# A hybrid decoder layer on one core: rows of x scaled before their transposes, dummy products ahead of the first unit, and two memory attention units moved between the heads of the differential attention

## The chip, the core and the metric

The kernel runs on one core of a Trainium2 chip. The core has a matrix engine (TensorE, PE in the profile, with its weight loads as PEld), a vector engine (DVE), a scalar engine (ACT), a general engine (POOL), and DMA queues issued mainly by SP. Each engine works through its own queue in order and waits on semaphores for the others. The metric is the device time of one launch in microseconds.

## The reference

One layer for 512 rows (tokens) of width 1024, in fp32. What the change touches is the beginning (the first norm and projection) and the two attention groups:

```python
h = rms_norm(x, attn_norm[l])
proj = h @ w_in[l]
q_da, k_da, v_da, rw_cols, q_mem = jnp.split(proj, [c1, c2, c3, c4], axis=-1)
...
o_da = diff_attention(q_da, k_da, v_da, positions, ...)     # 4 heads, 2 softmax maps each, causal
o_rw = rwkv7_time_mix(rw_cols, ...)                         # 4 heads, recurrent state
o_mem = memory_attention(q_mem, mem_n, w_mem_kv[l], ...)    # 4 heads on 256 memory rows
mixed = jnp.concatenate([o_da, o_rw.astype(o_da.dtype), o_mem], axis=-1)
x = x + mixed @ w_out[l]
xn = rms_norm(x, ffn_norm[l])
x = x + hierarchical_moe(xn, ...)                           # 16 experts of width 512
```

The norm is `x * rsqrt(mean(x*x) + eps) * gain`, by row.

## The kernel before

**Weights.** A stream (`WeightStream`) loads blocks of 512 KB into raw tiles; ACT rounds each to a high part (L96) and DVE subtracts it for a low part (L97). A product in fp32 accuracy is then three products of such parts (`mm3`, L243 to L245; in the first unit L341 to L343; in the output projection L1063 to L1065).

**The front.** x lies in four tiles `xt[0]` to `xt[3]` of 128 rows by 1024 (in the profile `f`). `row_root` gives 1/rms of each row: the sum of squares by DVE (L279) for tiles 0 and 2 and by ACT (L281) for tiles 1 and 3, then two POOL operations (L282, L283). DVE (tiles 0, 1, L348) and ACT (tiles 2, 3, L364) multiply the identity by the root, which gives a diagonal (in the profile `qmT`). `half_turn(n)` is two products of a 128x128 block of x with a diagonal (L328), which transpose and scale at once; n counts 16 half-blocks, the first 8 for tiles 0 and 1. They go to six PSUM banks, two half-blocks to a bank. `half_split(n)` reads a half-block into a high part (L291, ACT) and a low one (L292, DVE) with the norm's gain. `half_products` multiplies them with the first two weight blocks: 24 products of 128x256 for each group of four half-blocks. In this part the order on ACT, DVE and PE is the order in which it is written (`manual_schedule`); elsewhere a scheduler orders each engine's queue.

**The middle.** A weaver (`Weave`) interleaves generators by the costs that they yield: projections, the recurrence of RWKV (with a solve on DVE, L743 and L744, whose result goes through DRAM to the products L772), and attention.

**Attention.** `attention` runs through 20 units. A unit "d" is a block of 128 query rows of one head of the differential attention, in four sizes; a unit "m" is half the rows of a pair of memory heads, and a to d are the four of them. In step i the scores of unit i are issued, then the values of unit i−3, then the transposes of unit i−2. Scores of a memory unit are eight products (L949) into two PSUM banks `pp`, two reductions for the maxima (L952, DVE), four exponentials that read the banks (L956, ACT) and a scaling by POOL (L959). Its turn is eight transposes (L976) in two groups with a copy by ACT after each (L977), its values are four products (L1010). When a head is complete, its rows are normalized, transposed (L1003) and split (L291, L292). Then `out_first` begins the output projection (L1063 to L1065) in four `pp` banks; `give` hands two tiles of attention to the weight stream as further raw tiles. The 16 experts follow from about 340 us on.

Of the kernel before, what the change touches and what calls it, by code (L numbers as in the profile page):

```python
# [150 lines left out]
def hybrid_layer_kernel(ctx, tc, x, mem, positions, cols, w_in, w_kv, w_out, wa2, g2, ffn, wr, br,  # L151
# [22 lines left out]
    def pc():  # L174
        return pools["ps"].tile([P, 512], F32, name="pc", bufs=2)
# [18 lines left out]
    def b4(name, shape, dtype=F32):  # L194
        return biga.tile(shape, dtype, name=name)
# [79 lines left out]
    def row_root(src, vec=True):  # L275
        ss = wk.tile([P, 1], F32, name="ssx", bufs=4)
        r = wk.tile([P, 1], F32, name="rsx", bufs=4)
        if vec:
            V.tensor_tensor_reduce(b4("aw0", [P, D]), src, src, 1.0, 0.0, op0=ALU.mult, op1=ALU.add, accum_out=ss)  # L279
        else:  # L280
            A.activation(b4("aw1", [P, D]), src, AF.Square, accum_out=ss)  # L281
        G.tensor_scalar(r, ss, 1.0 / D, RMS_EPS, op0=ALU.mult, op1=ALU.add)  # L282
        return r, G.tensor_tensor(r, r, mhalf, op=ALU.pow)  # L283
# [9 lines left out]


    held = [ws.pair.pop() for _ in range(4)]
    ws.pump()
    for t in (2, 3):
        nc.sync.dma_start(xt[t], x[t * P:(t + 1) * P, :])
# [5 lines left out]
    dint = post_[:, S:2 * S]  # L304
    nc.sync.dma_start(posr, bass.AP(tensor=positions.tensor, offset=positions.offset, ap=[[0, P], [1, S]]))
    nc.sync.dma_start(posc, positions.rearrange("o (t p) -> p (o t)", p=P))
    diags = [b4(f"qmT{t}", [P, 2, P]) for t in range(2)]
    diag = [diags[t // 2][:, t % 2, :] for t in range(NT)]
    first_ps = [pp() for _ in range(2)]
    first_w = []  # L310

# [12 lines left out]
    def half_turn(n):  # L324
        hf, k = divmod(n, KC)
        o = half_bank(n)
        for t in range(2):
            T.matmul(o[:, t * P:(t + 1) * P], xt[2 * hf + t][:, k * P:(k + 1) * P], diag[2 * hf + t], start=True, stop=True)  # L328

    def half_split(n):  # L330
        hf, k = divmod(n, KC)
        tk = slice(hf * 256, hf * 256 + 256)
        return split_cols(half_bank(n), col[:, C_AN + k:C_AN + k + 1], h_hi[:, k, tk], h_lo[:, k, tk])
# [9 lines left out]
                T.matmul(o, wl, h_hi[:, k, tk], start=False, stop=k == KC - 1, skip_group_check=True)  # L343

    with tc.manual_schedule(engines={mybir.EngineType.Activation, mybir.EngineType.DVE, mybir.EngineType.PE}):
        roots = [row_root(xt[0]), row_root(xt[1], False)]
        for t in range(2):
            V.tensor_scalar(diag[t], ident, roots[t][0], None, op0=ALU.mult)  # L348
        for n in range(6):
            half_turn(n)  # L350
        weights()
        half_split(0)
        half_split(1)
        for n in (6, 7):
            half_turn(n)
        half_split(2)
        half_split(3)
        weights()
        roots += [row_root(xt[2]), row_root(xt[3], False)]
        half_products(0, range(4))  # L360
        for n in range(4, KC):
            half_split(n)
        for t in (2, 3):
            A.activation(diag[t], ident, AF.Copy, scale=roots[t][0])  # L364
        for n in range(KC, KC + 4):
            half_turn(n)
        half_products(0, range(4, KC))
        half_split(KC)
        half_split(KC + 1)
        for n in range(KC + 4, 2 * KC):  # L370
            half_turn(n)
        for n in range(KC + 2, 2 * KC):
            got_h = half_split(n)
        half_products(1, range(KC))
# [524 lines left out]
    def attention():  # L899
# [9 lines left out]
        aws = [b4("aw0", [P, 1024]), b4("aw1", [P, 1024])]  # L909
        obs = [b4("ob1", [P, S]), None]  # L910
        yield lambda: done[0] == 6
        units = [z for c in "0123abcd" for z in ([("d", int(c), qb) for qb in range(NT)] if c in "0123" else [("m", "abcd".index(c), 0)])]
        st = {}

        def scores(i):
# [102 lines left out]
            return None  # L1018

        n = len(units)  # L1020
        closes = {}
        for i in range(n + 3):
            if i == 1:
                yield has("bk_done")
                pr2 = b4("f0", [P, 2, 1024])
                prs[1:] = [pr2[:, k, :] for k in range(2)]
            elif i == 7:
                yield has("merged")
                obs[1] = b4("prod", [P, S])
            if i < n:  # L1030
                scores(i)
            if i == 15:
                with tc.high_priority(offset=GP):
                    ws.depth = 2 * DEPTH
                    give(("kT", 2), ("qT", 2))
                    ws.depth = DEPTH
            if i == n - 1:
                wv.spawn(out_first(), OUT_PRI)
            if i == 3:
                yield has("v0")  # L1040
            if i == 8:
                yield has("proj")
            if 0 <= i - 3 < n:
                cl = values(i - 3)
                if cl:
                    closes[i + 2] = cl
            if 0 <= i - 2 < n:
                turn(i - 2)
            if i in closes:
                closes.pop(i)()  # L1050
            yield (2.5 if i < 16 else 4.5)
        for k in sorted(closes):
            closes[k]()
        flags.add("att")
# [48 lines left out]
    with tc.issue_after(anchor[0].ins):  # L1103
# [4 lines left out]
        dum = rc.tile([P, 1], F32, name="dum")  # L1108
        G.iota(dum, pattern=[[0, 1]], base=S, channel_multiplier=1, allow_small_or_imprecise_dtypes=True)
        tri = rc.tile([P, P], BF, name="tri")  # L1110
        onb = rc.tile([P, P], BF, name="onb")
        G.memset(onb, 1.0)
        G.affine_select(tri, onb, pattern=[[1, P]], compare_op=ALU.is_gt, fill=0.0, base=0, channel_multiplier=-1)
        member = rc.tile([P, NT, NE], BF, name="member")
        rankm = rc.tile([P, NT, NE], F32, name="rankm")
# [387 lines left out]
```

## Time and profile before

| | us |
|---|---|
| median of 3 runs | 627.85 |
| lowest and highest | 626.47, 631.8 |
| the profiled execution | 631.21 |
| its span, first to last instruction | 629.5 |
| PE busy in it | 603.6 |
| DVE busy in it | 496.4 |
| ACT busy in it | 413.9 |

The rows of the trace come from one profiled execution. In a timeline row, the first number is the start and the second the duration in us, then engine, line, operation, output and inputs; x8 is a group of eight. In square brackets stands how long the engine was idle before it, and what ended that. PE's records overlap, so that a group's time divided by its count is a little more than the distance from one record to the next.

### The profile page before, as it was taken

The numbers are of one execution on the slowest core, as the hardware profiler recorded it, in microseconds if no ns is written. First come the engines' busy times: TensorE is split into PE (matmuls) and PEld (weight loads), VectorE is DVE, ScalarE is ACT, GpSimd is POOL, SyncE is SP. The second block draws the span as 40 slices with busy tenths as digits, with TensorE's granted clock in tenths as the row PEclk, the third lists the DMA queues.
The fourth block names the chain that finished last, engine by engine and source line by source line (L and its number), as shares of the span: only waits on it lengthen the run. The fifth ranks groups of instructions, "written<-read, shape, count | busy, mean of one in ns | idle before, by whom it ended". The sixth has DMA issues, their size and how long they took to land.

```text
span 629.5 us, 11197 instructions
## 1 busy us (share of the span) xinstructions
PE 603.6 (96%) x4130; PEld 486.6 (77%) x4130; DVE 496.4 (79%) x897; ACT 413.9 (66%) x633; POOL 124.0 (20%) x129
## 2 busy tenths in 40 slices
PE   4999999999999999999998999999999999999992
PEld 4968899999988877889996777777777777777771
DVE  5655795699966687555468999999999999988991
ACT  5478433453449675655247788888889888888881
POOL 2710211244400114304002011111011111320001
PEclk9999999999999997999999999999999999999997
DMA  9442333323252030879798999999999999799913
GB/s 303 137 137 67 101 101 98 87 70 99 68 118 69 2 135 1 298 272 348 278 336 278 364 345 371 372 373 355 364 356 361 363 364 373 232 373 375 337 26 54
DMA packets 77502, 144.19 MB, mean 229 GB/s; under 512 B 12832, under 2 KB 30496, under 8 KB 77440
## 3 DMA queue, kind: packets, MB, share of 16 engines
q1 hardware_dynamic: 69344, 126.59, 57.1%
q0 software_dynamic: 3760, 13.24, 8.9%
q10 hardware_dynamic: 4336, 3.57, 1.8%
q8 instruction: 34, 0.56, 0.4%
q14 instruction: 28, 0.23, 0.1%
HBM read 131.72 MB, written 11.67 MB: 228 GB/s over the span
## 4 chain that ended last, share of the span: by engine, by line
PE 82%; DVE 9%; DMA 3%; ACT 2%; issue 2%; POOL 1%; ACTq 0%; POOLq 0%; SPq 0%; DVEq 0%
PE pp L243 14%; PE pp L245 13%; PE pp L244 13%; PE py L244 5%; PE py L245 4%; PE py L243 4%; DVE prod L743 3%; DVE wlo L97 3%; PE pp L1063 3%; PE pp L1064 2%; PE pp L1065 2%; PE pt L986 2%; DVE lor L744 2%; PE pp L1345 1%; PE py L1201 1%
## 5 line engine op out<-in xcount | busy, mean ns | idle before, releaser
L245 PE MATMUL pp<-whi,xl 128*96 128x512 f32 x264 | 104.0, 395 | 0.0
L244 PE MATMUL pp<-wlo,xh 128*96 128x512 f32 x264 | 103.8, 394 | 0.0
L243 PE MATMUL pp<-whi,xh 128*96 128x512 f32 x264 | 101.2, 394 | 0.8 <-ACT xh L1332 0.8
L1393 POOL DMA_INDIRECT out<-ye,sidx x16 | 23.2, 1452 | 226.3 <-DVE gidx L1295 118.7
L96 ACT ACTIVATE whi<-raw 128x1024 fp32r<-128x1024 f32 x42 | 44.1, 1058 | 32.9 <-PE pp L245 24.7
L245 PE MATMUL pp<-whi,hm_l 128*128 128x256 f32 x224 | 63.8, 285 | 0.0
L243 PE MATMUL pp<-whi,hm_h 128*128 128x256 f32 x224 | 63.1, 282 | 0.0
L244 PE MATMUL pp<-wlo,hm_h 128*128 128x256 f32 x224 | 63.1, 282 | 0.0
L97 DVE TENSOR_TENSOR wlo<-raw,whi 128x1024 fp32r<-128x1024 f32 x42 | 53.7, 1284 | 11.2 <-ACT whi L96 10.8
L243 PEld LDWEIGHTS pp<-whi,xh 128*96 128x96 f32 x264 | 42.5, 161 | 19.6 <-ACT xh L1332 1.3
L245 PEld LDWEIGHTS pp<-whi,xl 128*96 128x96 f32 x264 | 42.6, 161 | 18.4
L244 PEld LDWEIGHTS pp<-wlo,xh 128*96 128x96 f32 x264 | 42.5, 161 | 18.2
L244 PE MATMUL py<-wlo,hh 128*96 128x512 f32 x120 | 47.9, 399 | 0.0
L245 PE MATMUL py<-whi,hl 128*96 128x512 f32 x120 | 47.0, 392 | 0.0
L243 PE MATMUL py<-whi,hh 128*96 128x512 f32 x120 | 47.0, 392 | 0.0
L97 DVE TENSOR_TENSOR wlo<-u,whi 128x1024 fp32r<-128x1024 f32 x34 | 40.8, 1224 | 6.2 <-ACT whi L96 6.1
L97 DVE TENSOR_TENSOR wlo<-lraw,whi 128x1024 fp32r<-128x1024 f32 x36 | 42.6, 1219 | 2.7 <-ACT whi L96 2.5
L245 PEld LDWEIGHTS pp<-whi,hm_l 128*128 128x128 f32 x224 | 42.1, 188 | 1.2 <-issue 0.5
L243 PEld LDWEIGHTS pp<-whi,hm_h 128*128 128x128 f32 x224 | 42.0, 188 | 1.0 <-DVE sm L936 0.4
L244 PEld LDWEIGHTS pp<-wlo,hm_h 128*128 128x128 f32 x224 | 42.3, 189 | 0.6 <-issue 0.2
L96 ACT ACTIVATE whi<-lraw 128x1024 fp32r<-128x1024 f32 x36 | 37.1, 1058 | 5.1 <-PE pp L245 3.6
L96 ACT ACTIVATE whi<-u 128x1024 fp32r<-128x1024 f32 x34 | 35.2, 1057 | 6.7 <-PE pp L1065 3.7
(405 smaller groups left out, 1568.5 us busy)
## 6 DMA issues: line engine op xcount, KB each, us to landing
raw<-in_w_in SPq DMA_DIRECT2D x22, 512.0 KB, 3.7
u<-in_wd SPq DMA_DIRECT2D x12, 512.0 KB, 9.4
lraw<-in_wg SPq DMA_DIRECT2D x12, 512.0 KB, 11.2
lraw<-in_wu SPq DMA_DIRECT2D x12, 512.0 KB, 7.5
lraw<-in_wd SPq DMA_DIRECT2D x12, 512.0 KB, 12.4
f<-in_wg SPq DMA_DIRECT2D x11, 512.0 KB, 10.0
u<-in_wu SPq DMA_DIRECT2D x11, 512.0 KB, 12.5
eraw<-in_wd SPq DMA_DIRECT2D x10, 512.0 KB, 13.5
```

Of the source, the lines that this page charges most:

```text
L96: nc.scalar.activation(hi, slot, AF.Copy)
L97: nc.vector.tensor_sub(lo, slot, hi.bitcast(F32))
L243: T.matmul(ps, ah, bh, start=first, stop=False)
L244: T.matmul(ps, ah, bl, start=False, stop=False)
L245: T.matmul(ps, al, bh, start=False, stop=last)
L743: V.tensor_mul(prod[:, :, 0:n], ud[:, s:s + 1, s:32].to_broadcast([P, 16, n]), zs[:, :, s:32])
L744: V.tensor_reduce(zs[:, :, s], prod[:, :, 0:n], axis=AX.X, op=ALU.add)
L986: T.matmul(po[:, 0:P], aws[i % 2][:, kb * P:(kb + 1) * P], qk["v"][:, kb, h * P:(h + 1) * P], start=kb == 0, stop=kb == qb)
L1063: T.matmul(o, ah, hi[:, k % 4, :], start=k == k0 and i == lead, stop=False, skip_group_check=True)
L1064: T.matmul(o, ah, lo[:, k % 4, :], start=False, stop=False, skip_group_check=True)
L1065: T.matmul(o, al, hi[:, k % 4, :], start=False, stop=k == k1, skip_group_check=True)
L1393: G.indirect_dma_start(out, bass.IndirectOffsetOnAxis(ap=si, axis=0), ye, None, compute_op=ALU.add)
```

## The change

Four things are changed. First, the two halves of each row of x are multiplied by the root in place (L354 by ACT for tiles 0 and 2, L355 by DVE for tiles 1 and 3), and `half_turn` is a transpose with the identity; the diagonals are gone. Second, 80 products of a 128x128 tile of ones in bf16 with itself (L348) stand at the head of PE's queue; nothing reads their result. The tile `onb` is set earlier on POOL for that. Third, the front's order: the roots of tiles 2 and 3 are written ahead of the second weight block's split, and the second half of the first half's products (`half_products(0, 4..7)`) ahead of the transposes 8 to 11. Fourth, the attention units go in the order 0, 1, a, 2, b, 3, c, d instead of 0, 1, 2, 3, a, b, c, d; the gift of `kT` and `qT` comes at the last unit "d" (step 17 instead of 15), and a step yields 2.5 for a unit "d" and 4.5 else. Lines behind the front are 7 to 9 higher after the change: L949 is L957, L976 is L984, L1010 is L1018, L1003 is L1011, L772 is L780, and L1063 to L1065 are L1072 to L1074.

```diff
--- before.py
+++ after.py
@@ -293,6 +293,8 @@
 
 
     held = [ws.pair.pop() for _ in range(4)]
+    onb = rc.tile([P, P], BF, name="onb")
+    G.memset(onb, 1.0)
     ws.pump()
     for t in (2, 3):
         nc.sync.dma_start(xt[t], x[t * P:(t + 1) * P, :])
@@ -304,8 +306,6 @@
     dint = post_[:, S:2 * S]
     nc.sync.dma_start(posr, bass.AP(tensor=positions.tensor, offset=positions.offset, ap=[[0, P], [1, S]]))
     nc.sync.dma_start(posc, positions.rearrange("o (t p) -> p (o t)", p=P))
-    diags = [b4(f"qmT{t}", [P, 2, P]) for t in range(2)]
-    diag = [diags[t // 2][:, t % 2, :] for t in range(NT)]
     first_ps = [pp() for _ in range(2)]
     first_w = []
 
@@ -325,7 +325,7 @@
         hf, k = divmod(n, KC)
         o = half_bank(n)
         for t in range(2):
-            T.matmul(o[:, t * P:(t + 1) * P], xt[2 * hf + t][:, k * P:(k + 1) * P], diag[2 * hf + t], start=True, stop=True)
+            T.transpose(o[:, t * P:(t + 1) * P], xt[2 * hf + t][:, k * P:(k + 1) * P], ident)
 
     def half_split(n):
         hf, k = divmod(n, KC)
@@ -343,28 +343,36 @@
                 T.matmul(o, wl, h_hi[:, k, tk], start=False, stop=k == KC - 1, skip_group_check=True)
 
     with tc.manual_schedule(engines={mybir.EngineType.Activation, mybir.EngineType.DVE, mybir.EngineType.PE}):
+        early = pc()
+        for _ in range(80):
+            T.matmul(early[:, 0:P], onb, onb, start=True, stop=True)
         roots = [row_root(xt[0]), row_root(xt[1], False)]
-        for t in range(2):
-            V.tensor_scalar(diag[t], ident, roots[t][0], None, op0=ALU.mult)
+
+        def half_scale(hf):
+            for i in range(2):
+                cs = slice(i * 512, i * 512 + 512)
+                A.activation(xt[2 * hf][:, cs], xt[2 * hf][:, cs], AF.Copy, scale=roots[2 * hf][0])
+                V.tensor_scalar(xt[2 * hf + 1][:, cs], xt[2 * hf + 1][:, cs], roots[2 * hf + 1][0], None, op0=ALU.mult)
+
+        half_scale(0)
         for n in range(6):
             half_turn(n)
         weights()
-        half_split(0)
-        half_split(1)
+        for n in range(2):
+            half_split(n)
         for n in (6, 7):
             half_turn(n)
-        half_split(2)
-        half_split(3)
+        for n in range(2, 4):
+            half_split(n)
+        roots += [row_root(xt[2]), row_root(xt[3], False)]
         weights()
-        roots += [row_root(xt[2]), row_root(xt[3], False)]
         half_products(0, range(4))
         for n in range(4, KC):
             half_split(n)
-        for t in (2, 3):
-            A.activation(diag[t], ident, AF.Copy, scale=roots[t][0])
+        half_scale(1)
+        half_products(0, range(4, KC))
         for n in range(KC, KC + 4):
             half_turn(n)
-        half_products(0, range(4, KC))
         half_split(KC)
         half_split(KC + 1)
         for n in range(KC + 4, 2 * KC):
@@ -909,7 +917,7 @@
         aws = [b4("aw0", [P, 1024]), b4("aw1", [P, 1024])]
         obs = [b4("ob1", [P, S]), None]
         yield lambda: done[0] == 6
-        units = [z for c in "0123abcd" for z in ([("d", int(c), qb) for qb in range(NT)] if c in "0123" else [("m", "abcd".index(c), 0)])]
+        units = [z for c in "01a2b3cd" for z in ([("d", int(c), qb) for qb in range(NT)] if c in "0123" else [("m", "abcd".index(c), 0)])]
         st = {}
 
         def scores(i):
@@ -1018,6 +1026,7 @@
             return None
 
         n = len(units)
+        last_d = max(i for i in range(n) if units[i][0] == "d")
         closes = {}
         for i in range(n + 3):
             if i == 1:
@@ -1029,7 +1038,7 @@
                 obs[1] = b4("prod", [P, S])
             if i < n:
                 scores(i)
-            if i == 15:
+            if i == last_d:
                 with tc.high_priority(offset=GP):
                     ws.depth = 2 * DEPTH
                     give(("kT", 2), ("qT", 2))
@@ -1048,7 +1057,7 @@
                 turn(i - 2)
             if i in closes:
                 closes.pop(i)()
-            yield (2.5 if i < 16 else 4.5)
+            yield 2.5 if i < n and units[i][0] == "d" else 4.5
         for k in sorted(closes):
             closes[k]()
         flags.add("att")
@@ -1108,8 +1117,6 @@
         dum = rc.tile([P, 1], F32, name="dum")
         G.iota(dum, pattern=[[0, 1]], base=S, channel_multiplier=1, allow_small_or_imprecise_dtypes=True)
         tri = rc.tile([P, P], BF, name="tri")
-        onb = rc.tile([P, P], BF, name="onb")
-        G.memset(onb, 1.0)
         G.affine_select(tri, onb, pattern=[[1, P]], compare_op=ALU.is_gt, fill=0.0, base=0, channel_multiplier=-1)
         member = rc.tile([P, NT, NE], BF, name="member")
         rankm = rc.tile([P, NT, NE], F32, name="rankm")
```

On PE, at the start of the program, there stood (`f` is x, `qmT` a diagonal, `pt`, `pc`, `pp` are PSUM banks, `whi` and `wlo` weights):

```order
L328 MATMUL pt<-qmT_132,f_96 128x128 x4
L328 MATMUL pc<-qmT_132,f_96 128x128 x4
L328 MATMUL pp<-qmT_132,f_96 128x128 x4
L328 MATMUL pt<-qmT_132,f_96 128x128 x4
L341 MATMUL pp<-hm_h,whi_80 128x256
L342 MATMUL pp<-hm_l,whi_80 128x256
```

and now stands, behind 78 more such products:

```order
L348 LDWEIGHTS onb
L348 MATMUL pc<-onb 128x128
L348 LDWEIGHTS onb
L348 MATMUL pc<-onb 128x128
L328 MATMUL pt<-ident,f_96 128x128 x4
L328 MATMUL pc<-ident,f_96 128x128 x4
L328 MATMUL pp<-ident,f_96 128x128 x4
L328 MATMUL pt<-ident,f_96 128x128 x4
L341 MATMUL pp<-hm_h,whi_80 128x256
L342 MATMUL pp<-hm_l,whi_80 128x256
```

The dummies are ahead of the transposes, which take the identity where the diagonal was.

On PE, around the scores of unit d (`mkT`, `qmT` are the memory's keys and queries), there stood:

```order
L949 MATMUL pp<-mkT_379,qmT_377 128x256 x3
L859 MATMUL pc<-f_990,u_648 64x64 x4
L845 MATMUL pc<-f_990,u_647 64x64 x8
L949 MATMUL pp<-mkT_379,qmT_377 128x256 x4
L854 MATMUL pc<-f_990,f_991 64x64 x4
L1003 MATMUL pt<-ident,ob_2004 128x128 x4
L986 MATMUL pt<-v_da,aw_2002 128x128 x3
L1063 MATMUL pp<-whi_85,hm_h 128x256
L1064 MATMUL pp<-wlo_86,hm_h 128x256
L1065 MATMUL pp<-whi_85,hm_l 128x256
L1063 MATMUL pp<-whi_80,hm_h 128x256
```

and now stands:

```order
L1018 MATMUL pt<-aw_2087,mv 64x256 x2
L1018 MATMUL pt<-aw_2088,mv 64x256 x2
L977 MATMUL pt<-ident,f_2251 128x128
L957 MATMUL pp<-mkT_464,qmT_462 128x256 x4
L862 MATMUL pc<-f_1075,f_1076 64x64 x4
L957 MATMUL pp<-mkT_464,qmT_462 128x256 x3
L994 MATMUL pt<-v_da,aw_2087 128x128
L977 MATMUL pt<-ident,pown 128x128 x2
L867 MATMUL pc<-f_1075,u_733 64x64 x4
L853 MATMUL pc<-f_1075,u_732 64x64 x8
L1072 MATMUL pp<-whi_85,hm_h 128x256
L1073 MATMUL pp<-wlo_86,hm_h 128x256
```

Of unit d's eight score products the last three now stand five rows ahead of the first output product (L1072), with small products of the recurrence and transposes of the last head (L977) in between; before, a head's transpose (L1003) and values (L986) stood there.

On PE, where units c and d are turned (`aw` is their transposed attention, `mv` the memory's values, L822 and L830 a transpose of the recurrence, `prod` a head's rows), there stood:

```order
L976 MATMUL pt<-ident,f_2166 128x128 x4
L1010 MATMUL pt<-aw_2002,mv 64x256 x2
L1010 MATMUL pt<-aw_2003,mv 64x256 x2
L976 MATMUL pt<-ident,pown 128x128 x4
L822 MATMUL pc<-ident,r_t 128x128 x4
L976 MATMUL pt<-ident,pown 128x128 x4
L1003 MATMUL pt<-ident,prod 128x128 x4
L1010 MATMUL pt<-aw_2002,mv 64x256 x2
L1010 MATMUL pt<-aw_2003,mv 64x256 x2
L1063 MATMUL pp<-whi_85,hm_h 128x256 x3
L1064 MATMUL pp<-wlo_86,hm_h 128x256 x3
```

and now stands:

```order
L830 MATMUL pc<-ident,r_t 128x128 x4
L994 MATMUL pt<-v_da,aw_2088 128x128 x4
L984 MATMUL pt<-ident,pown 128x128 x8
L1018 MATMUL pt<-aw_2087,mv 64x256 x2
L1018 MATMUL pt<-aw_2088,mv 64x256 x2
L984 MATMUL pt<-ident,f_2251 128x128 x8
L1018 MATMUL pt<-aw_2087,mv 64x256 x2
L1018 MATMUL pt<-aw_2088,mv 64x256 x2
L1011 MATMUL pt<-ident,prod 128x128 x4
L1072 MATMUL pp<-whi_85,hm_h 128x256 x4
L1073 MATMUL pp<-wlo_86,hm_h 128x256 x4
```

The turns and values of c and d and the closing transpose of the last head (L1011) are in one row, with output products only ahead of it and behind it.

## Rows read from the trace of the kernel before

**Rows 1.** The page: span, busy shares, TensorE clock by fortieths, last chain by engine

```profile
span 629.5 us, 11197 instructions
...
PE 603.6 (96%) x4130; PEld 486.6 (77%) x4130; DVE 496.4 (79%) x897; ACT 413.9 (66%) x633; POOL 124.0 (20%) x129
...
PEclk9999999999999997999999999999999999999997
...
PE 82%; DVE 9%; DMA 3%; ACT 2%; issue 2%; POOL 1%; ACTq 0%; POOLq 0%; SPq 0%; DVEq 0%
```

**Rows 2.** Waits of PE, 0 to 340 us: total, times, longest

```profile
PE pt L328 <- DVE qmT L348: 8.4, 2, 8.2
...
PE pc L772 <- DMA lor<-zs_d: 0.8, 1, 0.8
```

**Rows 3.** Timeline, 7 to 31 us: start, duration, engine, line

```profile
8.90 0.28 DVE L348 TENSOR_SCALAR qmT<-ident,rsx 128x128 f32<-128x128 f32 x1 [0.40 <-POOL rsx L283]
...
9.24 1.65 PE L328 MATMUL pt<-qmT,f 128*128 128x128 f32 x6 [0.21 <-DVE qmT L348]
...
9.57 1.23 DVE L97 TENSOR_TENSOR wlo<-raw,whi 128x1024 fp32r<-128x1024 f32 x1
10.07 0.47 ACT L291 ACTIVATE hm_h<-pt,col 128x256 fp32r<-128x256 f32 x1 [1.35 <-PE pt L328]
...
10.71 0.48 DVE L292 SCALAR_TENSOR_TENSOR hm_l<-pt,col,hm_h 128x256 fp32r<-128x256 f32 x1
...
13.74 1.06 PE L328 MATMUL pt<-qmT,f 128*128 128x128 f32 x8
...
14.56 0.36 PE L341 MATMUL pp<-hm_h,whi 128*128 128x256 f32 x1
...
23.14 1.05 PE L328 MATMUL pt<-qmT,f 128*128 128x128 f32 x8
...
30.46 0.28 PE L343 MATMUL pp<-hm_h,wlo 128*128 128x256 f32 x1
```

**Rows 4.** Two stretches of PE's timeline: a transpose group, and 128-column bf16 products

```profile
271.90 0.60 PE L976 MATMUL pt<-ident,f 128*128 128x128 f32 x4
...
321.83 0.66 PE L1269 MATMUL pp<-onb 128*128 128x128 bf16 x9
```

**Rows 5.** Groups by line and form, 186 to 290 us: count, busy us, mean ns

```profile
L977 ACT ACTIVATE aw<-pt 128x512 f32<-128x512 f32 x8 | 4.8, 595 | 1.5 <-PE pt L976 1.5
...
L1142 DVE TENSOR_TENSOR u<-pp,u 128x512 f32<-128x512 f32 x4 | 2.6, 684 | 3.2 <-PE pp L1065 3.2
```

**Rows 6.** Windows: PE, PEld, DVE, ACT, POOL busy (count), PEclk, DMA, GB/s

```profile
180.00:190.00 10.00, 9.21 (x101) 8.23 (x99) 4.88 (x18) 4.41 (x15) 1.04 (x2) 1.00 0.49 99
190.00:240.00 50.00, 50.00 (x611) 40.22 (x608) 38.00 (x123) 39.77 (x109) 6.83 (x9) 1.00 0.20 65
240.00:242.00 2.00, 0.89 (x10) 0.35 (x6) 1.97 (x5) 1.93 (x8) 1.58 (x1) 1.00 0.00 0
242.00:250.00 8.00, 8.00 (x44) 6.91 (x44) 4.80 (x15) 2.28 (x8) 2.86 (x2) 0.57 0.01 2
...
266.00:270.00 4.00, 3.34 (x26) 2.06 (x24) 3.01 (x7) 3.69 (x8) 0.00 (x0) 1.00 1.03 373
```

**Rows 7.** Timeline, 239 to 244 us, all engines

```profile
239.49 0.69 PE L845 MATMUL pc<-f,u 128*64 128x64 f32 x16
...
239.61 1.29 DVE L952 TENSOR_REDUCE mxm<-pp 128x2 f32<-128x512 f32 x2
...
239.99 0.47 ACT L956 ACTIVATE f<-pp,mxm 128x256 f32<-128x256 f32 x1
...
241.36 0.48 ACT L956 ACTIVATE f<-pp,mxm 128x256 f32<-128x256 f32 x1
...
243.94 0.93 PEld L854 LDWEIGHTS pc<-f,f 128*64 128x64 f32 x8 [0.65 <-DVE mxm L952]
```

**Rows 8.** Source view of L1063: count, duration min/median/max, first and last start

```profile
L1063 PE MATMUL pp<-xhi,hm_h x32: 276/276/364, 287.1 to 307.8; 128*128 128x256 f32 x32
```

## The prediction

> **What bounds the kernel now.** Read the page first [rows 1]: PE is busy 603.6 of 629.5 us, and 82% of the chain that ended last is PE. Then PE's waits [rows 2]: before 340 us the only long one is at the start, 8.2 us until the first diagonal L348; the next, 0.8 us, is at L772, for a DMA. So from about 14.5 us on the program is one long PE queue, and an edit is worth what it takes from that queue, from its few holes, or from stretches in which it runs at half pace. The rest is found in three places.
>
> The start [rows 3]: PE waits until the roots are known, then turns the first half of x by products with diagonals. [...] The first projection products run from 14.5 to 30.46 + 0.28 us. The end of attention [rows 6]: in 240–242 PE is busy 0.89 of 2 us; in 242–250 the granted clock is 0.57, so 0.43 × 8 = 3.4 us are lost; in 266–270 0.66 us are idle. And L772 [rows 6]: 180–190 has 0.79 us idle.
>
> **The change, part by part.** *Transposes for diagonal products.* A diagonal product of 128 columns leaves two records, a transpose one: 64 records become 32. Eight records of L328 take 1.05 us warm [rows 3]; four transposes of the same width take 0.60 [rows 4], and with the 0.27 us that the last one drains, that is 0.11 apart. Warm, 32 × 0.11 = 3.5 us leave PE's queue. At half pace, as the first 24 records ran, it is up to twice as much for those.
>
> *Scaling in place* takes the place of four 128-column diagonals. ACT: two halves of 512 columns at 0.60 (L977) [rows 5]. DVE: two at 0.69, from L1142, which reads two inputs of that size [rows 5]; four L348s of 0.28 [rows 3] would bound it above at 1.12 each, and below one diagonal itself, 0.28. I take 0.69, the nearest shape. The roots come as before, the second at 8.90, so the first transposes start at 8.90 + 0.69 = 9.6 instead of 8.2 and 9.24, and L97, which stood at 9.57, starts at 10.3 + and ends at 11.6.
>
> *The order of the front, by hand from these durations.* Transposes 0–5: 9.6 to about 11.1. Splits L291/L292 at 0.47 and 0.48 [rows 3] are now the limit: the first L292 follows L97 at 11.6, so the bank for transposes 6 and 7 is free at 12.6, and products 0–3 start at about 12.9, where before it was 14.5. They take 24 × 0.117 = 2.8 us, to 15.7. The square sum of x's third tile (taken as 1.23, L97's price for as many columns) and the second L97 stand on DVE ahead of splits 4–7, so products 4–7 wait until about 16.5 (0.8 us of new PE wait) and run to 19.3. DVE's second scaling ends there too; being ahead of transposes 8–11 on DVE but behind products 4–7 on PE, it is covered. Without that cover its 1.4 us would show. Sixteen transposes to 21.4, 48 products of 0.117 to about 27.1 + 0.5. Before, the last started at 30.46. The front gains **3.1 us**; 0.9 if the products run at half pace for a while (first rival), 3.7 if the transposes start at 9.2.
>
> *Eighty dummy products* of onb stand ahead of all this on PE. Warm, such products come (0.66 − 0.22)/8 = 0.055 apart [rows 4]; at half pace 0.11. PE begins near 1.5 us, as soon as POOL has made onb. All at full pace they take 4.4 us, half of them at each pace 40 × 0.11 + 40 × 0.055 = 6.6, to about 8.1, ahead of the first transpose at 9.6. All at half pace: 8.8 us, to 10.3, which delays the transposes by 0.7, of which the wait for L97 hides most. So they cost 0 to 0.5, taken as 0; what they give (full pace for transposes and products) is in the 3.1. The memset of onb was already there, and is moved on POOL ahead of nothing that waits.
>
> *The middle.* It is carried along by PE's queue. L772's wait for the solve's DMA may go or grow. In the new order L772 stands earlier by some 50 matmuls, but DVE has less to do during the solve (two weight splits and attention's first reductions come after it). I take the wait as gone: **−0.8**; bounds −0.8 and +3.1 (the front's whole gain waits there).
>
> *Memory units a and b among the heads, c and d at the end.* A unit's chain is two reductions (L952, 1.29 us for both) and four exponentials 0.47 apart (239.99 to 241.36 and 0.5 more) [rows 7], about 3.4 us before its two banks are free again. Before, four chains follow one another with little PE work between them, and this made the holes at 240–250. What may go: 1.1 (240–242), 0.65 (L854, waiting for L952 [rows 7]), 3.4 (half clock), 0.66 (266–270): **−5.8**. What comes: units a and b, each among score products of a head and the recurrence's small matmuls, which cover the chain wholly (0) or not at all (3.4); I take 0.7 each, near the low end, since the 0.89 busy in 240–242 stands at the third and fourth unit, and in 190–240, with the first two in it, PE is busy throughout [rows 6]. At the end the output products stand six PE rows behind unit d's fifth score and need a bank that unit c's exponentials free: 3.4 − 2.1 us of small matmuls between them (40 records, for which the L845 row gives 0.04 each, and some wider) = 1.3. Then transposes and values of c and d stand in one row with no output products between them (the third piece of the order): after each, PE waits for copies of 0.60 by ACT, and the closing transpose's split must end before the next products: 0.6 + 0.6 + 1.0 = 2.2; bounds 0.7 (before, 266–270) and 4. New: 1.4 + 1.3 + 2.2 = **+4.9**. The tail gives −0.9.
>
> *The later gift of kT and qT* (two more raw tiles for each) delays four weight loads by the time of two units. DMA is idle in 242–250 (share 0.01 [rows 6]), and the products that read the given tiles start only at 287.1 [rows 8]: taken at 0, at most the delay itself, 5 us, if that lead were used up.
>
> Sum: −3.1 − 0.8 − 0.9 = −4.8 against the profiled execution's 631.21, which is 626.4; that execution was 3.4 us above the median of the runs, so the median becomes 627.85 − 4.8 = **623.0 us**.
>
> [...] The traces show transposes only between other products (L976 above at 0.11, warm). [...]
>
> **Rivals.** (1) *Half pace returns in the front.* PE idles or only transposes from 8.1 to 12.9, and the products start at half pace as if the dummies were not there. A stretch at half pace like the one between 9.24 and 13.74 costs products 4.5 / 2 = 2.25 us; the front then gives 0.85, and the time is 627.85 − 0.85 − 0.8 − 0.9 = 625.3. For it: the clock is at 0.57 in 242–250, behind two us in which PE was busy for 0.89. Against: 266–270, with 0.66 us idle, shows 1.00 [rows 6]. (2) *The tail works as meant*: covers hold, a and b cost nothing, the last row 1: −5.8 + 1.0, so 627.85 − 3.1 − 0.8 − 4.8 = 619.1. For it: ACT and DVE are below 80% busy over the whole [rows 1]; against: 240–242 has both full. (3) *Slower: the convoy at the end of attention.* The row of c's and d's transposes stands in PE's order behind copies and splits that share ACT and DVE with the recurrence's closing steps. If each of its four hand-overs waits 2 us instead of 0.6, that is +8 in place of +3.5, and the half clock comes back over the first output products twice for a spell like 242–250 (+6.9). Then −3.1 − 0.8 − 5.8 + 1.4 + 8 + 6.9 = +6.6, so 634.4. It is slower from the point where new waits and spells pass 9.7 us. (4) *The front gain doesn't arrive*: the solve and its DMA set L772, PE just waits there longer: 627.85 − 0.9 = 626.9 and at worst 628. For it: the wait there now, 0.8; against: it is short, and DVE is given less before it.
>
> **How the numbers follow.** Forecast 0.35, (1) 0.18, (2) 0.24, (3) 0.09, (4) 0.14. A measurement of this kernel tells about 1% (6.3 us) from no change, so faster means under 621.6. Rival 2 is nearly all there (0.23), and of the forecast, whose own bounds are 619.5 to 627, about a third (0.12): 0.35. Slower needs over 634.1: half of rival 3 and a bit, 0.06. The rest, 0.59, is within 1%. The range leaves out the lower part of rival 2's own spread and rival 3: 617.5 to 629.
>
> **What will show it.** Rows of bf16 products from about 1.5 to 8.4 us, the last ones 0.055 apart; the first transposes at 9.6 and 0.11 apart; the front's last L343 near 27.3; L780 (L772 before) with no wait; the granted clock between 236 and 250 at 1.00; waits at L957 and L1018, and the last first-pass output product 4 to 6 us earlier than before. It is wrong if products at 13 us are 0.23 apart, if PE's wait ahead of L780 grows, or if a new low clock shows behind the row of c and d.

## The result, and the profile after

The changed kernel takes 623.07 us (median of 4 runs, 622.17 to 623.28), the kernel before 628.68 (4 runs, 626.47 to 631.8). The ratio is 0.9888, with a 95% interval of 0.9843 to 0.9933: faster by 1.1%. The profiled execution took 623.02 us. The runs of the kernel before spread five times as wide as those of the kernel after; its longer executions are those with more time at a lower granted TensorE clock (the mean is 0.988 at 631.21 us, in experiment 12 0.992 at 627.05, in 4 0.995 at 626.47), and a run more than 1.5% above the fastest of its kernel is left out of the ratios below.

The page of the changed kernel, its lines on span, busy shares, clock by fortieths and the chain that ended last, to hold against [rows 1]:

```profile
span 621.2 us, 11302 instructions
...
PE 600.6 (97%) x4178; PEld 484.3 (78%) x4178; DVE 498.1 (80%) x899; ACT 415.4 (67%) x635; POOL 123.1 (20%) x129
...
PEclk9999999999999999999999999999999999999997
...
PE 90%; DVE 4%; ACT 2%; DMA 2%; issue 1%; POOL 0%; POOLq 0%; ACTq 0%; DVEq 0%
```

The chain is now PE for 90%, against 82%; no fortieth of the clock line is below its highest digit up to the last. PE is busy 3 us less, though the dummies' 7.02 us are in it.

The waits of PE in 0 to 340 us (to hold against [rows 2]: total, times, longest):

```profile
PE pc L348 <- POOL onb L297: 1.2, 1, 1.2
PE pp L1072 <- ACT pp L1150: 1.2, 1, 1.2
PE pt L328 <- DVE hm_l L292: 1.1, 1, 1.1
...
PE pp L1072 <- ACT hm_h L291: 0.8, 1, 0.8
...
PE pt L1018 <- ACT aw L985: 0.5, 2, 0.4
PE pp L243 <- ACT f L964: 0.5, 1, 0.5
```

The 8.2 us at the start have become dummies, and the wait at the solve's products (L772, now L780) is not in the list. New are L1072 behind the square L1150, L1072 behind the last head's split, L1018 behind the copies of c and d, and a wait for a memory unit's exponentials (L964). L328 now waits 1.1 us for a split. No wait of PE for a DMA is among them, so the later gift of `kT` and `qT` shows no cost there.

The timeline of the front (start, duration), to hold against [rows 3]:

```profile
1.20 7.02 PE L348 MATMUL pc<-onb 128*128 128x128 bf16 x80 [1.20 <-POOL onb L297]
...
8.60 0.88 DVE L355 TENSOR_SCALAR f<-f,rsx 128x512 f32<-128x512 f32 x2 [1.27 <-POOL rsx L283]
...
9.53 0.60 PE L328 MATMUL pc<-ident,f 128*128 128x128 f32 x4
...
10.00 1.23 DVE L97 TENSOR_TENSOR wlo<-raw,whi 128x1024 fp32r<-128x1024 f32 x1 [0.16 <-ACT whi L96]
...
11.67 0.83 PE L328 MATMUL pt<-ident,f 128*128 128x128 f32 x4 [1.11 <-DVE hm_l L292]
...
12.26 0.36 PE L341 MATMUL pp<-hm_h,whi 128*128 128x256 f32 x1
12.46 0.28 PE L342 MATMUL pp<-hm_l,whi 128*128 128x256 f32 x1
12.58 0.28 PE L343 MATMUL pp<-hm_h,wlo 128*128 128x256 f32 x1
12.70 0.28 PE L341 MATMUL pp<-hm_h,whi 128*128 128x256 f32 x1
...
26.16 0.28 PE L343 MATMUL pp<-hm_h,wlo 128*128 128x256 f32 x1
26.28 0.40 PE L243 MATMUL pp<-hm_h,whi 128*128 128x512 f32 x1
```

The dummies run from 1.20 to 8.22, the transposes are (0.60 − 0.27)/3 = 0.11 apart, and L97 stands between the scaling and the first split as foreseen. The products follow each other 0.12 apart from the second on, which is full pace (at half pace, in 10, they come 0.21 apart). The scaling costs DVE 0.88 for two halves, not 1.38. The last product of the front starts at 26.16 instead of 30.46.

The end of attention, in one window (PE, PEld, DVE, ACT, POOL busy, clock, DMA share, GB/s); [rows 6] has parts of it for the kernel before:

```profile
236.00:250.00 14.00, 13.63 (x130) 11.59 (x127) 11.98 (x32) 9.42 (x31) 2.90 (x2) 1.00 0.89 323
```

PE is busy 13.63 of 14 us at a granted clock of 1.00.

Two landmarks on PE's timeline part the program in three: the first full-width product (L243 on h) and the first product of the experts (L243 on xh). All runs that were profiled, in us:

| kernel | first full-width product | first expert product | from one to the other |
|---|---|---|---|
| before (the profile shown) | 30.58 | 331.14 | 300.56 |
| before, second profile (4) | 30.31 | 326.27 | 295.96 |
| before, third profile (12) | 29.89 | 327.12 | 297.23 |
| **after** | 26.28 | 322.43 | 296.15 |
| 1 front only | 26.20 | 322.53 | 296.33 |
| 2 units only | 30.25 | 328.61 | 298.36 |
| 11 units only, again | 30.18 | 331.35 | 301.17 |
| 3 no dummies | 26.16 | 322.69 | 296.53 |
| 5 before with dummies | 28.92 | 327.70 | 298.78 |
| 6 turns only | 29.19 | 326.90 | 297.71 |
| 7 order only | 29.53 | 326.67 | 297.14 |
| 8 units 0a1b2c3d | 27.41 | 334.38 | 306.97 |
| 9 square aside | 26.73 | 321.80 | 295.07 |
| 10 units 012a3bcd | 26.29 | 322.33 | 296.04 |

Against the second profile of the kernel before, which has no low clock between the landmarks, the change gains 30.31 − 26.28 = 4.0 us in the front and loses 0.2 between the landmarks. The first landmark differs from one execution to the next: the old front has it at 29.89 to 30.58 in five executions (the three of the kernel before, 2 and 11), the changed front with dummies at 26.28 and 26.20, and the same front without dummies at 26.16 to 27.41 in four (3, 8, 9, 10).

### The profile page after: what moved, and what is told of

The parts are those of the page before. It is cut to its first block, busy times and chain, and to the rows that moved or that the text cites. A ratio compares the mean times of both kernels' runs of the same rounds, so it can differ in the third digit from the quotient of the medians.

```text
span 621.2 us, 11302 instructions
## 1 busy us (share of the span) xinstructions
PE 600.6 (97%) x4178; PEld 484.3 (78%) x4178; DVE 498.1 (80%) x899; ACT 415.4 (67%) x635; POOL 123.1 (20%) x129
## 4 chain that ended last, share of the span: by engine, by line
PE 90%; DVE 4%; ACT 2%; DMA 2%; issue 1%; POOL 0%; POOLq 0%; ACTq 0%; DVEq 0%
PE pp L243 17%; PE pp L245 17%; PE pp L244 16%; PE py L244 5%; PE py L245 4%; PE py L243 4%; PE pp L1072 3%; PE pp L1073 2%; PE pp L1074 2%; PE pt L994 2%; PE pp L1352 1%; PE py L1208 1%; DVE wlo L97 1%; PE pl L1175 1%; PE pc L687 1%; PE pp L1374 1%
## 5 line engine op out<-in xcount | busy, mean ns | idle before, releaser
L243 PE MATMUL pp<-whi,xh 128*96 128x512 f32 x264 | 101.2, 394 | 0.8 <-ACT xh L1339 0.8
L243 PE MATMUL pp<-whi,hm_h 128*128 128x256 f32 x224 | 64.4, 288 | 0.0
L97 DVE TENSOR_TENSOR wlo<-raw,whi 128x1024 fp32r<-128x1024 f32 x42 | 52.2, 1249 | 14.0 <-ACT whi L96 13.5
L243 PEld LDWEIGHTS pp<-whi,xh 128*96 128x96 f32 x264 | 42.5, 161 | 19.6 <-ACT xh L1339 1.3
L244 PEld LDWEIGHTS pp<-wlo,xh 128*96 128x96 f32 x264 | 42.5, 161 | 18.2
L243 PE MATMUL py<-whi,hh 128*96 128x512 f32 x120 | 47.0, 392 | 0.0
L97 DVE TENSOR_TENSOR wlo<-lraw,whi 128x1024 fp32r<-128x1024 f32 x36 | 42.6, 1217 | 2.8 <-ACT whi L96 2.7
L243 PEld LDWEIGHTS pp<-whi,hm_h 128*128 128x128 f32 x224 | 42.1, 188 | 2.0 <-issue 1.1
L97 DVE TENSOR_TENSOR wlo<-u,whi 128x1024 fp32r<-128x1024 f32 x34 | 41.2, 1234 | 3.1 <-ACT whi L96 3.0
## 6 DMA issues: line engine op xcount, KB each, us to landing
u<-in_wu SPq DMA_DIRECT2D x11, 512.0 KB, 12.9
```

What stands on the lines that cost most here:

```text
L97: nc.vector.tensor_sub(lo, slot, hi.bitcast(F32))
L243: T.matmul(ps, ah, bh, start=first, stop=False)
L244: T.matmul(ps, ah, bl, start=False, stop=False)
```

## The experiments

The theory: the front's gain is carried to the end by PE's queue; the new order of units gives a few us more at the end of attention. Rivals: the front's gain is lost at the solve; the dummies do nothing; the units do nothing or harm. Experiments 1 to 4, 5 to 8 and 9 to 12 ran on three chips, on each beside the kernel before, whose medians there are 627.75, 630.22 and 627.65 us; the ratios are to these.

**1 and 2. Either half alone.** In 1 the changed kernel has the old order of units, in 2 the kernel before has the new one:

```diff
-units = [z for c in "01a2b3cd" ...   # 1
+units = [z for c in "0123abcd" ...
-            if i == last_d:
+            if i == 15:
-            yield 2.5 if i < n and units[i][0] == "d" else 4.5
+            yield (2.5 if i < 16 else 4.5)
```

> The front of the changed kernel (scaling, transposes, dummies, order), attention units in the old order. Theory: the front's gain (4.3 us between the two traces at the first full-width product, 30.58 against 26.28) is carried by PE's queue to the end, less what L780 keeps: 2.5 to 4.3 us below the kernel before, ratio 0.993 to 0.996. Rival (the solve sets L780): PE waits there 3 us or more, ratio 0.998 to 1.000. The tail still has its holes at 236 to 246 and perhaps the low clock behind them.

> The old front, attention units in the order 01a2b3cd. Theory: the reordering alone gives 1 to 3.5 us (tail 1.7 and the waits at 172 and 187 1.8 between the two traces), ratio 0.994 to 0.998, and there is no low clock from 236 to 260. Rival: the tail's new waits (4.9 us) are all that it brings where the kernel before happens to run without its low clock, ratio 1.000 to 1.003.

1: 623.02 us (6 runs, 622.45 to 623.12), ratio 0.9921 [0.9905, 0.9937]. That is the changed kernel's time: the front is the whole gain, and it is carried to the end, as the theory says. The scheduler's plan behind the front is another one, though. A wait at 277 us that the kernel before lacks comes with the new front, in the old order of units:

```profile
PE pp L1072 <- ACT pp L1150: 1.4, 1, 1.4
```

2: 631.24 us (12 runs, 628.46 to 640.43; 629.88 for the nine in the ratio), ratio 1.0037 [1.0007, 1.0067]: by itself the new order is slower, by 0.4%. The theory's 1 to 3.5 us of gain fell, and the rival was nearer, with a loss somewhat larger than it gave. PE's waits in 2 (0 to 340 us):

```profile
PE pt L1010 <- ACT aw L977: 1.5, 3, 0.8
PE pp L1064 <- ACT pp L1144: 1.2, 1, 1.2
PE pp L1064 <- ACT pown L956: 0.9, 1, 0.9
```

Two of these waits are of the kind forecast for the changed kernel: copies of c and d (1.5) and a unit's exponentials (0.9). The wait for the block's square (1.2) was not forecast, and 1 has it too. Between the landmarks 2 takes 298.36 − 295.96 = 2.4 us more than the kernel before in 4.

**3. No dummies.**

```diff
-        early = pc()
-        for _ in range(80):
-            T.matmul(early[:, 0:P], onb, onb, start=True, stop=True)
```

> The changed kernel without the 80 dummy products. Theory: PE starts at half pace at 8.5 us, transposes come 0.22 to 0.24 apart, and the first products are at half pace until about 14; the first full-width product starts at 27.3 to 28.5 instead of 26.28, and the time is 1 to 2.2 us above the changed kernel. Rival: the transposes' waits for splits hide the slow pace, the first full-width product is within 0.5 us of 26.28 and the time within 0.5 us.

622.85 us (4 runs, 622.3 to 623.8), the changed kernel's time; the first full-width product is at 26.16. The rival holds in the time and in this execution. PE's timeline:

```profile
8.27 0.48 PE L328 MATMUL pt<-ident,f 128*128 128x128 f32 x1 [8.27 <-ACT f L351]
...
9.65 1.06 PE L328 MATMUL pc<-ident,f 128*128 128x128 f32 x4
10.51 1.06 PE L328 MATMUL pp<-ident,f 128*128 128x128 f32 x4
...
11.49 0.83 PE L328 MATMUL pt<-ident,f 128*128 128x128 f32 x4
12.08 0.36 PE L341 MATMUL pp<-hm_h,whi 128*128 128x256 f32 x1
12.28 0.28 PE L342 MATMUL pp<-hm_l,whi 128*128 128x256 f32 x1
12.40 0.28 PE L343 MATMUL pp<-hm_h,wlo 128*128 128x256 f32 x1
12.52 0.28 PE L341 MATMUL pp<-hm_h,whi 128*128 128x256 f32 x1
```

The transposes begin at half pace, 0.21 from one to the next (10.51 − 9.65 = 0.86 for four). The last four take 12.08 − 11.49 = 0.59 (in 10, at half pace to the end, 0.76), so the pace rises within them, and the products from 12.28 on come 0.12 apart: full pace. (The windows view prints a clock of 1.00 from 8 to 12 us all the same, so the pace is read from the distances of the records.)

That is one execution. 8, 9 and 10 below have the same front without dummies, and there the products start at half pace, 0.21 apart, up to 15.2, 14.2 and 13.3 us. From the timeline of 10:

```profile
12.65 0.41 PE L342 MATMUL pp<-hm_l,whi 128*128 128x256 f32 x1
12.87 0.41 PE L343 MATMUL pp<-hm_h,wlo 128*128 128x256 f32 x1
13.08 0.39 PE L341 MATMUL pp<-hm_h,whi 128*128 128x256 f32 x1
```

Their first full-width products are at 27.41, 26.73 and 26.29, later than in 3 by 1.25, 0.57 and 0.13; of this the transposes' later start is 0.48, 0.11 and 0.04. So dummies can save up to 0.8 us at the landmark in single executions. In the medians it does not show: 623.07 and 623.02 with dummies (the changed kernel and 1), 622.85 and 622.96 without (3 and 10).

**4 and 12. The kernel before, profiled twice more**, unchanged.

> The kernel before, profiled once more. Theory: the stretch at half clock at 242 to 249 us is not in every execution, and its presence is most of the 5 us between the fastest and slowest run of the kernel before: here either clock 0.988 with that stretch and a time near 630 to 632, or a clock of 0.993 or more without it and a time of 626 to 628. Rival: the stretch is always there and the runs differ elsewhere, so the granted clock at 242 to 250 is again about 0.57 whatever the time.

> The kernel before, profiled a third time. Theory: as for the look before it, a time over 630 comes with a stretch at half clock between 236 and 250 us, a time under 628 with none there; the part up to the first full-width product is within 0.3 us of 30.3 either way. Rival: time and clock do not go together.

4 took 626.47 us, 12 took 627.05. The window 236 to 250, first of 4, then of 12:

```profile
236.00:250.00 14.00, 12.90 (x132) 10.94 (x131) 10.34 (x28) 8.92 (x29) 7.25 (x5) 1.00 0.09 24
```

```profile
236.00:250.00 14.00, 12.89 (x121) 10.67 (x118) 9.63 (x26) 7.46 (x26) 5.72 (x5) 0.88 0.02 4
```

PE is busy 12.90 and 12.89 of 14 us in both, but the granted clock is 1.00 in the one and 0.88 in the other, which loses 14 × 0.12 = 1.7 us; the execution with which the prediction worked had 0.57 in 242–250 [rows 6] and lost 3.4. From landmark to landmark the three take 295.96, 297.23 and 300.56. The theory holds in kind: it is the same work with or without a low clock. Two of the expectations for 12 missed: it took under 628 us with a stretch of low clock in it, half as long as that of the first profile, and its first full-width product, at 29.89, is 0.4 us from 30.3. The other runs on record agree: of the 17 of the kernel before beside experiments 1 to 4, the two with the highest mean clock, 0.995, took 626.21 and 627.31 us, the two with the lowest, 0.985, 632.18 and 631.61. The wait at L772 and the one at 172 are not in every execution either: in 4 and 12 PE's idle time in 180–190 is 0.1 and 0.

**5, 6 and 7. Parts of the front on the kernel before**: 5 has the dummies alone (the three lines above, onb set earlier); 6 has scaling and transposes in the old order, without dummies and with the old units; 7 has the order alone, with diagonals:

```diff
-        weights()                                    # 7 (6 is the changed front with these undone)
         roots += [row_root(xt[2]), row_root(xt[3], False)]
+        weights()
...
+        half_products(0, range(4, KC))
         for n in range(KC, KC + 4):
             half_turn(n)
-        half_products(0, range(4, KC))
```

> The kernel before with the 80 dummy products ahead of its diagonal products, nothing else. Theory: in the kernel before the first 24 diagonal records are PE's own limit and come 0.24 to 0.28 apart; at full pace they take half of that, so the first full-width product starts 1 to 2 us earlier than at 30.3, the more so as splits and L97 on DVE then set the pace, and the time falls by 0.5 to 1.5 us (ratio 0.997 to 0.999, which this measurement hardly tells from 1). Rival: DVE's chain L97 and L292 was the limit there too, the first full-width product stays within 0.4 us of 30.3.

> Rows scaled in place and real transposes, but the old order of the front, no dummies, old order of units. Theory: 32 records of 0.11 to 0.24 us leave PE, which makes up most of the front's 4.1 us: first full-width product at 27 to 28 instead of 30.3, ratio 0.993 to 0.996. Rival: the gain hangs on the order (products 4 to 7 ahead of transposes 8 to 11); without it PE waits for the second scaling on DVE as long as the transposes save, first full-width product at 29 or later, ratio 0.998 or more.

> The kernel before with only the front's order changed: roots of tiles 2 and 3 ahead of the second weight block, products 4 to 7 ahead of transposes 8 to 11; diagonals as before. Theory: little, since before PE had no long wait there (0.5 us at L364): first full-width product between 29.8 and 30.6, ratio 0.999 to 1.001. Rival: the order is worth 1 us or more by itself.

The medians are 627.73, 627.76 and 627.04 us (12 runs each), with ratios 0.9964 [0.9931, 0.9996], 0.9966 [0.9939, 0.9993] and 0.9958 [0.9927, 0.9988] to 630.22 (35 runs of the kernel before, 626.34 to 639.86). The fastest runs are 626.46, 626.87 and 626.33: none clearly below the fastest of the kernel before. The landmark says 28.92, 29.19 and 29.53, so the parts give 1.4, 1.1 and 0.8 us against 30.31 (the last two little more than the old front itself varies), and without the dummies the two others together give 2.9 to 4.15 (27.41 to 26.16), against 1.9 for their sum. At the landmark the theory of 5 holds, that of 6 (27 to 28) falls, and 7 lies between its theory and its rival. In 6 the rival is right at the landmark: PE's transposes 8 to 11 stand ahead of products 4 to 7 and wait for the second scaling (POOL, DVE and PE rows):

```profile
16.96 0.95 POOL L390 MEMSET aw<- 128x1024 f32 x1
17.05 2.44 DVE L352 TENSOR_SCALAR f<-f,rsx 128x512 f32<-128x512 f32 x2 [0.15 <-POOL rsx L283]
...
17.30 0.33 PE L328 MATMUL pc<-ident,f 128*128 128x128 f32 x1 [0.69 <-ACT f L351]
...
19.00 0.55 PE L328 MATMUL pc<-ident,f 128*128 128x128 f32 x3 [1.36 <-DVE f L352]
```

Besides, the products of 6 run at half pace, 0.21 apart, from 12.7 up to 14.5 us, without dummies. In 7 it is the diagonal products that hold back all that follows, at half pace up to 12.21 and beyond (eight records from 10.51 to 12.21, 0.21 apart):

```profile
8.18 2.53 PE L328 MATMUL pt<-qmT,f 128*128 128x128 f32 x8 [8.18 <-DVE qmT L348]
...
12.21 1.70 PE L328 MATMUL pp<-qmT,f 128*128 128x128 f32 x8
...
14.56 0.36 PE L341 MATMUL pp<-hm_h,whi 128*128 128x256 f32 x1
```

Eight records take 2.53 with a wait in it, and the first product starts at 14.56. Only with both does PE have products to do while DVE scales, and half as many records of L328 ahead of the first product. What the parts gain at the landmark is partly lost again behind it (297.1 to 298.8 against 295.96): 5 has 1.7 us of low clock there and two waits, 0.8 and 0.8, at 171 and 185, and 6 and 7 have the wait of 1.4 us for the block's square that 1 has.

**8 and 10. Other places for the units**, on the kernel of 3: `"0a1b2c3d"` and `"012a3bcd"` for `"01a2b3cd"`.

> The changed kernel without dummies and with one memory unit behind each head (0a1b2c3d). Theory: with c among the heads only d is left at the end, so the row of c's and d's transposes and copies (about 2.5 us of waits between 257 and 263) is halved and PE's other holes stay: 0.5 to 1.5 us below the changed kernel, 621.5 to 622.5. Rival: the holes move to the heads (each unit's reductions and exponentials delay a head's), same or slower: 623 to 626.

> The changed kernel without dummies, with only unit a moved in among the heads (012a3bcd). Theory: with the new front the order of the units matters little as long as at least two units lie behind the last head: between the old order and the changed one, 622.5 to 623.5. Rival: each order lands on its own plan of the scheduler, as 0a1b2c3d did, and the time differs by more than 2 us either way.

10: 622.96 us (5 runs), as expected. 8: 634.0 us (10 runs, 632.51 to 640.49), ratio 1.0083 [1.0042, 1.0123]: against the theory, and worse than the rival's 623 to 626. Windows of 8:

```profile
190.00:195.00 5.00, 3.65 (x52) 3.10 (x51) 3.53 (x7) 4.95 (x13) 1.89 (x1) 1.00 0.00 2
195.00:200.00 5.00, 5.00 (x58) 3.88 (x57) 2.13 (x7) 2.15 (x7) 0.00 (x0) 0.62 0.70 208
...
268.00:272.00 4.00, 1.58 (x12) 0.62 (x8) 2.13 (x8) 1.33 (x4) 1.62 (x2) 0.91 0.97 312
272.00:276.00 4.00, 3.55 (x16) 3.56 (x17) 3.11 (x3) 2.87 (x4) 0.00 (x0) 0.50 0.99 352
```

PE idles 1.35 us at 190–195 (a head's scores wait for a reduction, L935) and 2.4 us at 268–272, and behind both the clock is at 0.62 and 0.50. So the order of units can cost ten us (306.97 against 296.53 between the landmarks), though the orders 0123abcd, 012a3bcd and 01a2b3cd come to the same.

**9. The square aside.** The largest new wait at the end of attention is PE's at 277 for a bank that ACT's square still holds (L1150). On the kernel of 3 it writes elsewhere:

```diff
-        A.activation(ps, x1c, AF.Square, accum_out=sqs[:, t, i:i + 1])
+        junk = rt.tile([P, 512], F32, name="junk", bufs=1)
+        A.activation(junk[:, 0:n], x1c, AF.Square, accum_out=sqs[:, t, i:i + 1])
```

> The changed kernel without dummies, and with the square of the residual rows (L1150 in the changed kernel) written to an SBUF tile that nothing reads instead of back into the PSUM bank. Theory: the 1.35 us in which PE waits at 277 for the first bank of the second pass is DVE's addition (0.69) and then ACT's square (0.58) that holds the bank; with the square aside PE waits 0.6 to 0.8, and the time is about 0.6 us below the changed kernel without dummies (622.3 against 622.85), which this measurement hardly tells. Rival: the bank is then held by something else, or the square is later and delays routing; the wait stays at 1.35.

621.41 us (6 runs, 620.72 to 622.04), ratio 0.9904 [0.9881, 0.9927]; beside it, on the same chip, 10 took 622.96 (622.2 to 623.6). This version beats both kernels. PE's waits in 260 to 290 no longer have the bank in them:

```profile
PE pp L1069 <- ACT hm_h L291: 0.8, 1, 0.8
PE pt L981 <- DVE hm_l L1020: 0.4, 1, 0.4
```

The wait went wholly, 1.35 us, not by half as the theory had it. 3 itself, on another chip, took 622.85.

**11. Units only, again.**

> The old front with the new order of units, profiled again. Theory: its times of 628 to 640 are executions with and without stretches at half clock between 180 and 290 us; a time over 631 comes with a granted clock below 0.99 and such a stretch, a time of 628 to 629 with none. Rival: the clock is the same and the long executions wait elsewhere.

631.46 us at a granted clock of 0.988. The stretch is there, and elsewhere than in the kernel before:

```profile
202.00:204.00 2.00, 2.00 (x37) 1.72 (x35) 1.45 (x9) 1.64 (x5) 1.01 (x1) 1.00 0.00 0
204.00:206.00 2.00, 2.00 (x29) 1.81 (x25) 1.20 (x4) 1.95 (x8) 0.35 (x1) 0.79 0.04 8
206.00:208.00 2.00, 2.00 (x16) 1.63 (x14) 1.17 (x4) 0.81 (x4) 1.55 (x2) 0.50 0.00 0
...
210.00:212.00 2.00, 2.00 (x17) 1.67 (x13) 0.97 (x5) 0.63 (x2) 0.00 (x0) 0.51 0.00 0
212.00:214.00 2.00, 2.00 (x17) 1.54 (x17) 1.12 (x4) 1.36 (x5) 0.40 (x1) 1.00 0.00 0
```

Half clock from about 205 to 212, though PE was busy 2.00 of 2 us in each window before. From landmark to landmark it took 301.17, 2.8 more than 2 did. The theory holds for this execution; those of 635 to 640 were not profiled, but their mean clocks are on record, 0.988 to 0.973.

## Why the prediction was right, and where its steps were not

The time (623.0 forecast, 623.07 measured) and the direction are right; the path to it is right in the front, and the sum was partly luck.

*The front*, forecast 3.1, measured 4.0 to 4.1. The mechanism is the forecast one: 32 records fewer, L97 ahead of the first split, products 4 to 7 over the second scaling. Mis-sized was the scaling on DVE, 0.44 each where 0.69 was taken; so the first product came at 12.26 instead of 12.9, and the new wait for splits 4 to 7 (0.8) is 0.5 in 1 and 0.2 in the changed kernel. The split of the gain was not seen: neither turns nor order give half of it (6, 7).

*The dummies*: cost 0, as forecast; but "what they give is in the 3.1" is not borne out by the times, which are the same without them (3, 10). On the timeline they give what was meant, full pace from the first products on, and the first rival is excluded by the changed kernel's own rows: the products come 0.12 apart from 12.46 on. Without dummies its half pace does come, in three executions of four (8, 9, 10), but it costs at most 0.8 us at the landmark, not the 2.25 that the rival took from the stretch up to 13.74 in the kernel before (eight records from 10.68 to 12.39 there, 0.21 apart): it ends by 15.2, and in 3 PE waits 0.4 us for a split behind the first products, a wait that the slower start of 10 takes up. In 3, PE did nothing but transposes from 8.27 to 12.08, at half pace up to the last four (0.59 us from 11.49 on, against 0.86 for four at 9.65), and the products behind them ran at full pace, 0.12 apart. So in 3 the pace rose while PE did transposes alone; in 8, 9 and 10 the transposes were over before it rose. Why it rose early in the one and late in the others was not shown.

*The middle*, forecast −0.8: the wait at L772 is gone, but a usual execution of the kernel before has hardly any (0.1 and 0 in 4 and 12). The step failed in taking one execution's wait for the kernel's.

*The tail*, forecast −0.9 from −5.8 and +4.9. From start to start on PE, less the usual distance, the changed kernel loses 0.6 at 220 behind a memory unit's exponentials and 0.5 at 240 behind the recurrence (L864); 1.4 was forecast for a and b. It loses 0.6 + 0.5 + 0.4 + 0.9 = 2.4 in the row of c and d and the closing transpose (forecast 2.2). The 1.3 forecast for a bank that unit c's exponentials hold did not come (2 has such a wait, 0.9). There is 1.35 at 277 before L1072, but that it has this size is luck: the bank is held by the block's square, and 1, 6 and 7 have this wait with the old order of units. What was to go was mis-sized: 3.4 of the 5.8 was the low clock of one execution. Against a usual execution the reordering gives nothing (1 against the changed kernel: 623.02 and 623.07), and rival 2 is excluded. What rival 3 feared, waits of 2 us and the half clock back twice, shows in 8, not here; rival 4 is refuted by 1.

So the number was luck in this way: against 4, the execution of the kernel before without a low clock (626.47), the changed kernel is 3.4 us shorter (4.0 in the front, less 0.2 between the landmarks and 0.4 behind them), 1.4 less than the forecast 4.8; and the median from which the 4.8 was taken, 627.85, lies 1.4 above that execution.

Of the measured 5.6 us between the medians, 4.0 are from the front, and lowest run against lowest run gives 4.3. The rest, about 1.6, is put down to stretches at low clock that pull up the median of the kernel before; this is argued from the three profiled executions and the clocks on record, not shown run by run. The 4 runs of the changed kernel and the 21 of 1, 3, 9 and 10 have no such long ones (each kernel's lie within 1.6 us). Nor has 7: its 12 runs lie within 1.7 us, where 35 of the kernel before on the same chip go from 626.34 to 639.86. So neither dummies nor scaling nor the order of units is needed for it; the front's order, with the other plan that the scheduler makes behind it, is enough. Which wait in that plan spares the long executions was not settled.

## What to carry to other kernels

A stall or a low clock in one profiled execution is a term of the sum only if other executions have it too: hold the profiled time against the fastest run first, and profile again where they differ. The same holds for one profiled execution of a variant: 3 alone would have said that the dummies change nothing on PE. Warm-up products in front of a stage gained little here, where PE soon waits for another engine (0.4 us for a split in 3): at most 0.8 us in single executions and nothing in the medians. And when two engines limit a stage in turn, two edits that look like 1 us each (1.1 and 0.8 in 6 and 7) can be worth three to four together (2.9 to 4.15 here), so try them together before judging either. An edit in one place can also change the plan of a scheduler far behind it; hold the waits there against each other, too.

## What the runs showed that was not expected

DVE's second scaling took 1.90 us for a half that elsewhere takes 0.48 (6: two halves in 2.44 us at 17.05, beside a POOL memset of 0.95 at 16.96 and others up to 18.2); the changed kernel has the same 2.44 at 16.58, under the products. And the clock in 11 fell to 0.50 at about 205 with no idle time of PE ahead of it: behind two groups of 32x32 products, 32 each (1.19 us from 201.08 and from 203.32). The same kernel in 2 has the same groups at 201.14 and 203.38 and no low clock there, so they are not enough to explain it.
